# A two-layer hybrid mLSTM / attention kernel: mLSTM scalings moved to ScalarE and joined from PSUM, a front with plain transposes, whole weight quarters and no GpSimd in its norm

## The chip, the cores and the metric

The kernel runs on one core of a Trainium2 chip. Its engines are TensorE (PE in the profile, with its weight loads as PEld), VectorE (DVE), ScalarE (ACT), GpSimd (POOL) and SyncE (SP), which here only issues DMAs. Each engine takes its own instructions in program order and waits on semaphores. The metric is the device time of one execution in microseconds (us); lower is better. Before the change it is 1554.34 us (median of 3 runs, 1553.78 to 1555.73).

## What is computed

Two layers run on 1152 tokens of 1024 features: 1024 latent tokens and 128 context tokens. All arithmetic is float32.

```python
hs = rmsnorm(x, g_pre) * (1 + scale(c)) + shift(c)     # shift, scale, gate = silu(c) @ w_mod + b_mod
# even layer: one projection p = hs @ w_in gives q, k, v, o, gates of 4 mLSTM heads, GQA's q, k, v, and z
h_f = mlstm_scan(q, k, v, ig_f, fg_f)                   # chunks of 128 tokens; h_b the same, reversed
#   in a chunk: P = exp(Dm - m_t) * (q k^T), Dm[l, s] = b_l - b_s + li_s for s <= l, else -inf
#   num = w_inter * (C q) + P v ; den likewise ; h = num / max(|den|, exp(-m_t))
#   C <- a * C + sum_s wk_s v_s k_s^T
ha = rmsnorm(h_f + h_b, g_hn) * sigmoid(o)
y = concat(ha, gqa) * silu(z) ; x = x + gate * rmsnorm(y @ w_out, g_post)
# odd layer: the same frame around neighbourhood attention
```

## The kernel before

**Products.** Projections keep float32 accuracy by splitting each operand into a high and a low part (`hh`, `hl` of the activations; `whi`, `wlo` of the weights) and adding three products in one PSUM bank (lines 371 to 373, 386 to 388, destination `pj`). `split` (line 108) makes the parts: ScalarE casts the high part (line 114), GpSimd or VectorE subtracts it to get the low one (line 115). Tokens lie in three chunks of 384 columns.

**The front** (`run`, from line 1295). The activations come transposed (`xT`, three chunks). For each of 8 feature blocks `mod_first` makes shift and scale: `mod_group` multiplies SiLU(c) by 1 MB of `w_mod` (line 198) and copies the 128x256 result `acc` out of PSUM by `evac`, which takes ScalarE and VectorE in turn (lines 101, 103); two products with a 128x2 selection matrix turn it (line 209); VectorE adds the bias (211, 212). `rms_cols` squares the chunk (290), adds the blocks (297), averages over partitions on TensorE (302), takes the power -1/2 on GpSimd (305) and spreads the row over all partitions by three float32 products with the identity (307). `norm_cols` forms `full` on VectorE (322), `hh` on ScalarE (326) and `hl` on VectorE (327); for the blocks listed in `pool` it takes another way: ScalarE adds the shift (324), ScalarE casts `hh` (114) and GpSimd subtracts (115). While chunk 0 is normalised block by block, the products of the gates (413, 414) and of four weight blocks accumulate in five PSUM banks. The four weight blocks come in quarters of 256 columns: `quarter` issues one DMA for each block (four of 128 KB, line 1332), `cut` splits the four pieces, low parts on GpSimd. SP issues the DMAs in the order of the code: `xT` of chunk 0, `w_mod` of block 0, quarter 0, the gate weights, then `w_mod` of blocks 1 to 7 with a quarter ahead of every second one.

**The mLSTM phase.** A planner of the framework sets the order of each engine's instructions from the code. For each head `mlstm` runs eight state updates: `kw` scales k by a column of `nat`, both directions, on GpSimd (670); TensorE multiplies it with v into the one bank `o` (673); VectorE updates the state `cs` (680). Then come three groups of three chunks. `decays` makes the weights `e` of a group from a broadcast of M: A - M for both directions on GpSimd (653, 128x768), the causal mask on GpSimd (`affine_select`, 656, fill -1e30), exp on ScalarE (658). VectorE multiplies `wb` by q (706) and `e` by the scores (711); TensorE forms the two directions' numerators and denominators in two banks `s` (717, 719); ScalarE takes |den| (725), VectorE floors and inverts it (728, 729), scales both banks into `hs` and `hb` (732, twice 128x384) and adds them (733). ScalarE squares (736), GpSimd takes the root (133, 134) and scales `hs` (739), TensorE transposes it (106), VectorE multiplies by the gate (750). Beside this the projections of the next heads run (`blocks`), and VectorE works off `mods_rest`: 128 reductions of 128x512 (line 252) for the other modulation vectors. The gates of a head: tanh on ScalarE (609), (tanh + 1) * g on GpSimd (610).

**SiLU.** `silu_gate` (390 to 397) makes silu(z) = z * (0.5 * tanh(z/2) + 0.5): tanh on ScalarE (395), the scaling on GpSimd (396), the product on VectorE (397), which frees the PSUM bank `pj` (two of them).

**Softmaxes.** The GQA, neighbourhood and context softmaxes end with a multiplication by 1/sum on GpSimd (924, 1275, 1036).

Of the kernel before, what the change touches and what calls it, by code (L numbers as in the profile page):

```python
# [39 lines left out]
class Kern:  # L40
# [150 lines left out]
    def mod_group(self, ws):  # L191

        nc = self.nc
        pm = self.ps("pj")
        for q, wm in enumerate(ws):
            for kk in range(4):
                b = 32 * kk
                nc.tensor.matmul(pm[b : b + 32, :256], self.cT[:, 4 * q + kk, :], wm[:, kk, :], start=q == 0, stop=q == 1, tile_position=(0, b))
        acc = self.st([P, 256], n="acc")
        self.evac(acc, pm[:, :256])  # L200
        return acc, pm[:, 256:260]

    def mod_first(self, k, ws):

        nc = self.nc
        m = self.mod0[:, k]
        acc, p2 = self.mod_group(ws)
        for j in range(2):
            nc.tensor.matmul(p2[:, 2 * j : 2 * j + 2], acc[:, j * P : (j + 1) * P], self.sel, start=True, stop=True)
# [74 lines left out]
    def rms_cols(self, xt, first=False):  # L284
# [21 lines left out]
        for i in range(3):  # L306
            nc.tensor.matmul(pt[:, i * P : (i + 1) * P], rs[:, i : i + 1].to_broadcast([P, P]), self.ident, start=True, stop=True)
# [4 lines left out]
    def norm_cols(self, h, c, xt, rms, ks, pool=()):

        nc = self.nc
        sh, sc = self.shift[0], self.scale[0]
        for k in ks:
            x, r1 = xt[k // 3][:, k % 3], rms[k > 0 or c > 0]
            f = self.t("full", 4, [P, CW])
            hh, hl = self.act(h, k, c)
            for r, s in ((0, slice(0, CW)),) if c < 2 else ((0, slice(0, 2 * P)), (1, slice(2 * P, CW))):  # L320
                s1, s2 = sc[:, k, r : r + 1], sh[:, k, r : r + 1]
                nc.vector.scalar_tensor_tensor(f[:, s], x[:, s], s1, r1[:, s], ALU.mult, ALU.mult)
                if k in pool:
                    nc.scalar.activation(f[:, s], f[:, s], AF.Identity, bias=s2)
                else:
                    nc.scalar.activation(hh[:, s], f[:, s], AF.Identity, bias=s2)
                    nc.vector.scalar_tensor_tensor(hl[:, s], f[:, s], s2, hh[:, s].bitcast(F32), ALU.add, ALU.subtract)
# [37 lines left out]
    def feat_part(self, ps, h, w, c, ks):  # L365
        nc = self.nc
        whi, wlo = w
        for k in ks:
            hh, hl = self.act(h, k, c)
            a, b = whi[:, k * P : (k + 1) * P], wlo[:, k * P : (k + 1) * P]  # L370
            nc.tensor.matmul(ps[:, :CW], a, hh, start=k == 0, stop=False)  # L371
# [1 line left out]
            nc.tensor.matmul(ps[:, :CW], b, hh, start=False, stop=k == KB - 1)  # L373
# [17 lines left out]
    def silu_gate(self, out, ps):  # L391

        nc = self.nc
        th = self.st([P, CW], n="th")
        nc.scalar.activation(th, ps, AF.Tanh, scale=0.5)
        nc.gpsimd.tensor_scalar(th, th, 0.5, 0.5, ALU.mult, ALU.add)
        nc.vector.tensor_tensor(out, th, ps, ALU.mult)  # L397

# [167 lines left out]
    def mlstm_proj(self, hd):  # L566
# [38 lines left out]
        def oev(c, ps):  # L605
            if c == 0:
                o["g"] = new("gate")
            g = o["g"][:, c * CW : (c + 1) * CW]
# [1 line left out]
            nc.gpsimd.tensor_scalar(g, g, 1.0, self.ghn[:, hd : hd + 1], ALU.add, ALU.mult)  # L610

# [35 lines left out]
    def decays(self, hd, g, t):  # L647

        nc = self.nc
        e, wb = t[:, 0:2], t[:, 2:4]  # L650
# [1 line left out]
        av = self.nat[:, 0, 3 * g : 3 * g + 3, :].rearrange("p c (d h) -> p h d c", d=2)[:, hd]
        nc.gpsimd.tensor_tensor(ev, av[:, :, :, None].to_broadcast([P, 2, 3, P]), ev, ALU.subtract)
        for d in range(2):
            s = 1 if d == 0 else -1
            nc.gpsimd.affine_select(out=ev[:, d], in_=ev[:, d], pattern=[[0, 3], [s, P]], compare_op=ALU.is_ge, fill=NEG, base=0, channel_multiplier=-s)
        ef = e.rearrange("p d l -> p (d l)")
        nc.scalar.activation(ef, ef, AF.Exp)
        return e, wb

    def mlstm(self, hd, cs, order, qT, kT, k, v, gt):
# [4 lines left out]
        def update(chs):  # L666

            kw = self.t("kw", 2, [P, 2, P])
            for d in range(2):
                nc.gpsimd.tensor_tensor(kw[:, d, :], k[:, chs[d], :], nat[:, 1, chs[d], 4 * d + hd : 4 * d + hd + 1].to_broadcast([P, P]), ALU.mult)  # L670
# [32 lines left out]
        for g in range(NC):  # L703
# [25 lines left out]
            nc.vector.reciprocal(den[:, :6], den[:, :6])  # L729
            for d in range(2):  # L730
                pv = po[d][:, : 3 * P1].rearrange("p (c l) -> p c l", l=P1)
                nc.vector.tensor_tensor((hs, hb)[d], pv[:, :, 0:P], den[:, 3 * d : 3 * d + 3, None].to_broadcast([P, 3, P]), ALU.mult)
            nc.vector.tensor_tensor(hs, hs, hb, ALU.add)
# [5 lines left out]
            nc.gpsimd.tensor_tensor(hs, hs, rs[:, :3, None].to_broadcast([P, 3, P]), ALU.mult)
# [282 lines left out]
    def ctx_steps(self, S, V, tmp, po=None, banks=("tr", "s")):  # L1022
# [13 lines left out]
        nc.gpsimd.tensor_tensor(pr, pr, r[:, :2, None].to_broadcast([P, 2, P]), ALU.mult)  # L1036
# [256 lines left out]
    def run(self):  # L1293
# [11 lines left out]
        with self.phase("front"):  # L1305
# [19 lines left out]
            take(0)  # L1325
            raws = [self.raw(), self.raw()] + [self.t(f"raw{b}", 1, [P, D]) for b in range(NB - 2)]
            w = [(self.u([P, D], F32R, "whi"), self.u([P, D], F32R, "wlo")) for _ in range(NB)]

# [25 lines left out]
            for k in range(KB):
# [283 lines left out]
```

## Time and profile before

| | |
|---|---|
| runs | 1554.34 us median, 1553.78 to 1555.73 |
| the profiled execution | 1554.8 us, its span 1553.0 us, mean granted TensorE clock 0.995 |
| busy in the span | PE 1499.3 us, PEld 1380.9, DVE 846.4, ACT 653.0, POOL 609.9 |
| chain that ended last | PE 83% of the span, DVE 6%, DMA 3%, POOL 2%, ACT 2% |
| moved by DMA | 143.80 MB |

Rows of groups read: line, engine, operation, destination<-sources, shapes, count | busy us, mean ns of one | idle time of the engine just before them and what ended most of it. Rows of waits read: engine, destination and line that waited <- engine, destination and line that ended the wait: us in total, times, the longest. Rows of stretches read: from:to in us, length, then for each engine busy us and the number of instructions, the granted clock, the DMA share and GB/s. A busy PE is not PE at its peak, since matmuls are pipelined and their ends are modelled.

### The profile page before, as it was taken

Reading aid. Unit: us, or ns where it says so; the run is one execution under the profiler, and the core shown is the slowest. Engines: PE = TensorE matmul, PEld = TensorE weight load, DVE = VectorE, ACT = ScalarE, POOL = GpSimd, SP = SyncE. Lnnn points to the kernel's source line nnn. Section 1 sums busy time; section 2 is a strip of 40 time slices with the busy share of each in tenths; the row PEclk is TensorE's granted clock in tenths of the full one; section 3 lists DMA queues with packets and bytes.
Section 4 is the critical chain, followed back from the end, with each engine's and each line's share of the span. In section 5 each row is a group of like instructions: output and inputs, shape, how many; then the busy total and the mean of one; then the engine's idle time right before and its main releaser. Section 6 shows DMA issues by size and latency. Waiting matters only on the chain.

```text
span 1553.0 us, 27156 instructions
## 1 busy us (share of the span) xinstructions
PE 1499.3 (97%) x10164; PEld 1380.9 (89%) x10164; DVE 846.4 (55%) x2342; ACT 653.0 (42%) x1573; POOL 609.9 (39%) x830
## 2 busy tenths in 40 slices
PE   7899999999999899999999999999999999999998
PEld 5799998999999888777788989999999999989886
DVE  5732997974547856665465452435243434345532
ACT  4622212112235767778344452445243434345411
POOL 3414645644445835577133332333142314243200
PEclk9999999999999999999999999999999999999999
DMA  9212634431220000021334212131213121225342
GB/s 354 81 42 102 219 124 182 158 113 65 104 93 32 17 23 32 24 72 49 134 108 159 74 52 87 34 105 27 90 44 97 31 84 39 87 76 151 128 130 82
DMA packets 75011, 143.80 MB, mean 93 GB/s; under 512 B 15928, under 2 KB 46848, under 8 KB 74880
## 3 DMA queue, kind: packets, MB, share of 16 engines
q1 hardware_dynamic: 70294, 126.91, 24.7%
q10 hardware_dynamic: 4586, 15.16, 2.6%
q8 instruction: 80, 1.31, 0.3%
q14 instruction: 51, 0.42, 0.1%
HBM read 115.47 MB, written 21.86 MB: 88 GB/s over the span
## 4 chain that ended last, share of the span: by engine, by line
PE 83%; DVE 6%; DMA 3%; POOL 2%; ACT 2%; issue 2%; SPq 0%; DVEq 0%; POOLq 0%; ACTq 0%
PE pj L371 12%; PE pj L373 12%; PE pj L372 12%; PE pj L386 7%; PE pj L387 7%; PE pj L388 7%; PE s L914 4%; PE ptr L106 4%; PE o L954 4%; PE o L1288 4%; PE s L1265 3%; PE tr L106 3%; DVE mj L252 2%; PE pj L106 2%; DMA wm<-in_w_mod_dram 1%
## 5 line engine op out<-in xcount | busy, mean ns | idle before, releaser
L371 PE MATMUL pj<-hh,whi 128*128 128x384 f32 x1168 | 399.9, 342 | 2.9 <-DVE z L397 2.5
L373 PE MATMUL pj<-hh,wlo 128*128 128x384 f32 x1168 | 396.9, 340 | 0.0
L372 PE MATMUL pj<-hl,whi 128*128 128x384 f32 x1168 | 396.0, 339 | 0.0
L371 PEld LDWEIGHTS pj<-hh,whi 128*128 128x128 f32 x1168 | 219.9, 188 | 6.1 <-DVE z L397 2.8
L372 PEld LDWEIGHTS pj<-hl,whi 128*128 128x128 f32 x1168 | 220.0, 188 | 1.3
L373 PEld LDWEIGHTS pj<-hh,wlo 128*128 128x128 f32 x1168 | 219.8, 188 | 1.2 <-issue 0.5
L115 POOL TENSOR_TENSOR wlo<-raw,whi 128x1024 fp32r<-128x1024 f32 (+1 forms) x75 | 156.4, 2096 | 154.6 <-ACT whi L114 105.8
L1275 POOL TENSOR_SCALAR sb<-sb,sm 128x512 f32<-128x512 f32 (+1 forms) x128 | 84.7, 667 | 242.6 <-DVE sm L1274 234.1
L924 POOL TENSOR_SCALAR pr<-pr,smg 128x384 f32<-128x384 f32 x192 | 109.2, 585 | 81.3 <-PE pj L106 41.9
L386 PE MATMUL pj<-whi,hh 128*128 128x256 f32 x432 | 122.5, 284 | 0.3 <-DVE nr L789 0.3
L387 PE MATMUL pj<-wlo,hh 128*128 128x256 f32 x432 | 122.5, 284 | 0.0
L388 PE MATMUL pj<-whi,hl 128*128 128x256 f32 x432 | 122.4, 283 | 0.0
L915 DVE CUSTOM_DVE_ANT_0 pr<-s,zero 128x384 f32<-128x384 f32 x192 | 103.6, 553 | 25.1 <-PE s L914 21.6
L386 PE MATMUL pj<-whi,yh 128*128 128x512 f32 x288 | 114.2, 397 | 2.1 <-DVE o L1083 1.5
L387 PE MATMUL pj<-wlo,yh 128*128 128x512 f32 x288 | 113.8, 395 | 0.0
L388 PE MATMUL pj<-whi,yl 128*128 128x512 f32 x288 | 113.4, 394 | 0.0
L252 DVE CUSTOM_DVE_ANT_0 mj<-wm,cb 128x512 f32<-128x512 f32 x128 | 110.8, 865 | 3.8 <-DMA wm<-in_w_modT_dram 1.8
L1273 ACT ACTIVATE sb<-sb,sm 128x512 f32<-128x512 f32 (+1 forms) x128 | 88.8, 695 | 51.6 <-DVE sm L1271 47.2
L914 PE MATMUL s<-Kst,Q 128*128 128x384 f32 x384 | 107.6, 372 | 0.7 <-DVE smg L915 0.7
L114 ACT CAST whi<-raw 128x1024 fp32r<-128x1024 f32 (+1 forms) x89 | 81.1, 930 | 22.9 <-DMA raw<-in_w_out_dram 6.6
L1271 DVE CUSTOM_DVE_ANT_1 sb<-s,bias 128x512 f32<-128x512 f32 (+1 forms) x112 | 72.9, 664 | 25.0 <-PE ptr L106 14.4
L386 PEld LDWEIGHTS pj<-whi,hh 128*128 128x128 f32 x432 | 81.3, 188 | 1.4 <-issue 0.5
(351 smaller groups left out, 2955.7 us busy)
## 6 DMA issues: line engine op xcount, KB each, us to landing
wm<-in_w_modT_dram SPq DMA_DIRECT2D x32, 512.0 KB, 5.9
raw<-in_w_c_dram SPq DMA_DIRECT2D x25, 512.0 KB, 3.6
raw<-in_w_ab_dram SPq DMA_DIRECT2D x20, 512.0 KB, 3.5
e<-rbd ACTq DMA_DIRECT2D x12, 768.0 KB, 5.5
bias<-in_na_bias_dram SPq DMA_DIRECT2D x16, 576.0 KB, 4.8
wm<-in_w_mod_dram SPq DMA_DIRECT2D x16, 512.0 KB, 7.0
raw<-in_w_out_dram SPq DMA_DIRECT2D x16, 512.0 KB, 3.6
y<-yd SPq DMA_DIRECT2D x18, 448.0 KB, 3.4
```

The source lines that it names most:

```text
L106: self.nc.tensor.transpose(out, in_, self.ident)
L115: (eng_lo or nc.gpsimd).tensor_tensor(lo, src, hi.bitcast(F32), ALU.subtract)
L252: nc.vector.tensor_tensor_reduce(junk, w[:, b, :], cb[:, r, :], 1.0, 0.0, ALU.mult, ALU.add, mp[:, hf, q // 4, 2 * (q % 4) + b, r : r + 1])
L371: nc.tensor.matmul(ps[:, :CW], a, hh, start=k == 0, stop=False)
L372: nc.tensor.matmul(ps[:, :CW], a, hl, start=False, stop=False)
L373: nc.tensor.matmul(ps[:, :CW], b, hh, start=False, stop=k == KB - 1)
L386: nc.tensor.matmul(ps[:, :width], hh, a, start=k == 0, stop=False)
L387: nc.tensor.matmul(ps[:, :width], hh, b, start=False, stop=False)
L388: nc.tensor.matmul(ps[:, :width], hl, a, start=False, stop=k == KB - 1)
L914: nc.tensor.matmul(s[:, :CW], x, y, start=part == 0, stop=part == 1)
L915: nc.vector.tensor_tensor_reduce(pr[:, c, :], s[:, :CW], zero, -1.0, -NEG, ALU.add, ALU.min, m3[:, c : c + 1])
L924: nc.gpsimd.tensor_scalar(pr[:, c, :], pr[:, c, :], r, 1.0, ALU.mult, ALU.mult)
```

## The change

Two sets of edits, in one kernel.

In the mLSTM phase: (1) `decays` gives ScalarE the whole of exp(A - M): six activations of 128x128 with a bias column and scale -1 in place of the one of 128x768, and the mask follows on GpSimd with fill 0. (2) `kw` is made by two ScalarE activations with a scale column. (3) The two directions are joined from PSUM: ScalarE scales the backward one into `hb` (three of 128x128), and VectorE multiplies the forward one and adds `hb` in one operation (three of 128x128). (4) `hs` is scaled by the root on ScalarE (three of 128x128). (5) (tanh + 1) * g becomes one ScalarE activation of 128x384. (6) `silu_gate` leaves out the halving: VectorE multiplies (tanh + 1) by z straight from PSUM, and the factor 0.5 goes into `ghn` (0.25) and into the 1/sum of the three softmaxes; for the context softmax this is one more VectorE operation of 128x2 (`ctx_steps`).

In the front: (7) the products with the selection matrix and with the identity become plain transposes (`flipped`), and the four row groups of the turned `acc` are added by one `tensor_reduce` on VectorE; `acc` is always copied by ScalarE. (8) The four weight blocks are stored in DRAM by quarters (`w_first`), so that one DMA of 512 KB brings a quarter and one cast and one subtraction split it, the subtraction on VectorE. (9) `norm_cols` has no GpSimd way any more.

```diff
 def mod_group(self, ws):
-        self.evac(acc, pm[:, :256])
-        return acc, pm[:, 256:260]
+        nc.scalar.copy(acc, pm[:, :256])
+        return acc, pm[:, 256:]
 def mod_first(self, k, ws):
-            nc.tensor.matmul(p2[:, 2 * j : 2 * j + 2], acc[:, j * P : (j + 1) * P], self.sel, start=True, stop=True)
+            self.flipped(p2[:, j * P : (j + 1) * P], acc[:, j * P : (j + 1) * P])
+        nc.vector.tensor_reduce(m, p2.rearrange("p (j g r) -> p j r g", j=2, r=32)[:, :, 0:2], AX.X, ALU.add)
-        nc.vector.tensor_tensor(m, p2.rearrange("p (b r) -> p b r", r=2), bias, ALU.add)
+        nc.vector.tensor_tensor(m, m, bias, ALU.add)
 def rms_cols(self, xt, first=False):
-            nc.tensor.matmul(pt[:, i * P : (i + 1) * P], rs[:, i : i + 1].to_broadcast([P, P]), self.ident, start=True, stop=True)
+            self.flipped(pt[:, i * P : (i + 1) * P], rs[:, i : i + 1].to_broadcast([P, P]))
 def norm_cols(...):
-                if k in pool:
-                    nc.scalar.activation(f[:, s], f[:, s], AF.Identity, bias=s2)
-                else:
-                    ...
-            if k in pool:
-                self.split(hh, hl, f)
+                nc.scalar.activation(hh[:, s], f[:, s], AF.Identity, bias=s2)
+                nc.vector.scalar_tensor_tensor(hl[:, s], f[:, s], s2, hh[:, s].bitcast(F32), ALU.add, ALU.subtract)
 def silu_gate(self, out, ps):
-        nc.gpsimd.tensor_scalar(th, th, 0.5, 0.5, ALU.mult, ALU.add)
-        nc.vector.tensor_tensor(out, th, ps, ALU.mult)
+        nc.vector.scalar_tensor_tensor(out, th, 1.0, ps, ALU.add, ALU.mult)
 def oev(c, ps):
-            nc.gpsimd.tensor_scalar(g, g, 1.0, self.ghn[:, hd : hd + 1], ALU.add, ALU.mult)
+            nc.scalar.activation(g, g, AF.Identity, scale=self.ghn[:, hd : hd + 1], bias=self.ghn[:, hd : hd + 1])
 def decays(self, hd, g, t):
-        nc.gpsimd.tensor_tensor(ev, av[:, :, :, None].to_broadcast([P, 2, 3, P]), ev, ALU.subtract)
         for d in range(2):
-            nc.gpsimd.affine_select(... fill=NEG ...)
-        nc.scalar.activation(ef, ef, AF.Exp)
+            for i in range(3):
+                nc.scalar.activation(ev[:, d, i], ev[:, d, i], AF.Exp, bias=self.nat[:, 0, 3 * g + i, 4 * d + hd : 4 * d + hd + 1], scale=-1.0)
+            nc.gpsimd.affine_select(... fill=0.0 ...)
 def update(chs):
-                nc.gpsimd.tensor_tensor(kw[:, d, :], k[:, chs[d], :], nat[...].to_broadcast([P, P]), ALU.mult)
+                nc.scalar.activation(kw[:, d, :], k[:, chs[d], :], AF.Identity, scale=nat[...])
 def mlstm(...):
-            for d in range(2):
-                nc.vector.tensor_tensor((hs, hb)[d], pv[:, :, 0:P], den[:, 3 * d : 3 * d + 3, None].to_broadcast([P, 3, P]), ALU.mult)
-            nc.vector.tensor_tensor(hs, hs, hb, ALU.add)
+            for i in range(3):
+                nc.scalar.activation(hb[:, i, :], b, AF.Identity, scale=den[:, 3 + i : 4 + i])
+                nc.vector.scalar_tensor_tensor(hs[:, i, :], f, den[:, i : i + 1], hb[:, i, :], ALU.mult, ALU.add)
...
-            nc.gpsimd.tensor_tensor(hs, hs, rs[:, :3, None].to_broadcast([P, 3, P]), ALU.mult)
+            for i in range(3):
+                nc.scalar.activation(hs[:, i, :], hs[:, i, :], AF.Identity, scale=rs[:, i : i + 1])
 def ctx_steps(...):
+        nc.vector.tensor_scalar(r[:, :2], r[:, :2], 2.0, None, ALU.mult)
 def run(self):
             def quarter(q):
-                for b in range(NB):
-                    nc.sync.dma_start(raws[b][:, o], a["w_ab"][b][:, o])
+                nc.sync.dma_start(raws[q], a["w_first"][q])
             def cut(q):
-                for b in range(NB):
-                    self.split(w[b][0][:, o], w[b][1][:, o], raws[b][:, o])
+                self.split(*w[q], raws[q].rearrange("p (b f) -> p b f", b=NB), eng_lo=nc.vector)
```

The order changes with it. GpSimd's instructions while the first head's output groups are formed (`sm` is the root of the norm, `e` the next head's decays, `wlo` low weights of a projection that runs beside), before:

```order
L656 AFFINE_SELECT e_1557<-e_1557 128x384 x2
L134 TENSOR_TENSOR sm_1553<-sm_1553,mhalf 128x3
L115 TENSOR_TENSOR wlo_1911<-raw_1908,whi_1910 128x1024
L739 TENSOR_TENSOR hs_1540<-hs_1540,sm_1553 128x384
L610 TENSOR_SCALAR gate_1833<-gate_1833,ghn 128x384
L653 TENSOR_TENSOR e_1612<-nat,e_1612 128x768
L133 TENSOR_SCALAR sm_1608<-sm_1604 128x3
```

and after, in the same place (the line numbers are those of the changed file):

```order
L133 TENSOR_SCALAR sm_1522<-sm_1518 128x3
L134 TENSOR_TENSOR sm_1522<-sm_1522,mhalf 128x3
L650 AFFINE_SELECT e_1528<-e_1528 128x384 x2
L115 TENSOR_TENSOR wlo_1892<-raw_1889,whi_1891 128x1024
L650 AFFINE_SELECT e_1588<-e_1588 128x384 x2
L133 TENSOR_SCALAR sm_1582<-sm_1578 128x3
```

GpSimd keeps the root, the mask and the low weights; the scaling of `hs`, the gate and the subtraction of the decays are gone from its queue. ScalarE's instructions in that place, before:

```order
L736 ACTIVATE hb_1541,sm_1549<-hs_1540 128x128 x3
L609 ACTIVATE gate_1833<-pj_1808 128x384
L725 ACTIVATE sm_1594<-s_1580 128x3
L114 CAST whi_1910<-raw_1908 128x1024
L725 ACTIVATE sm_1594<-s_1581 128x3
L644 DMA e_1612<-rbd 128x1536
L658 ACTIVATE e_1557<-e_1557 128x768
L609 ACTIVATE gate_1833<-pj_1842 128x384
```

and after:

```order
L724 ACTIVATE hb_1507<-s_1492,sm_1505 128x128 x3
L687 COPY ct_1473<-tr_1470 128x256
L728 ACTIVATE hb_1507,sm_1518<-hs_1506 128x128
L688 DMA out_dram<-ct_1473 128x2x128
L728 ACTIVATE hb_1507,sm_1518<-hs_1506 128x128 x2
L603 ACTIVATE gate_1814<-pj_1789 128x384
L717 ACTIVATE sm_1565<-s_1551 128x3
L649 ACTIVATE e_1528<-e_1528,nat 128x128 x2
L604 ACTIVATE gate_1814<-gate_1814,ghn 128x384
L649 ACTIVATE e_1528<-e_1528,nat 128x128 x4
L114 CAST whi_1891<-raw_1889 128x1024
L732 ACTIVATE hs_1506<-hs_1506,sm_1522 128x128 x3
```

ScalarE now takes `hb` from PSUM, the exponentials, the gate's scaling and `hs` between the copies (`gate`, `whi`) that it made before. VectorE's instructions in the front, where the first blocks of chunk 0 are normalised, before:

```order
L304 TENSOR_SCALAR sm_267<-ptr_257 128x3
L211 TENSOR_TENSOR mod_109<-pj_232,par 128x4
L212 SCALAR_TENSOR_TENSOR mod_109<-mod_109,par 128x2
L103 COPY acc_292<-pj_283 128x256
L322 SCALAR_TENSOR_TENSOR full_298<-xT_130,mod_109,ptr_257 128x384
L211 TENSOR_TENSOR mod_109<-pj_283,par 128x4
```

and after:

```order
L305 TENSOR_SCALAR sm_256<-ptr_246 128x3
L210 TENSOR_REDUCE mod_109<-pj_220 128x4
L212 TENSOR_TENSOR mod_109<-mod_109,par 128x4
L213 SCALAR_TENSOR_TENSOR mod_109<-mod_109,par 128x2
L115 TENSOR_TENSOR wlo_147<-raw_154,whi_146 128x1024
L323 SCALAR_TENSOR_TENSOR full_282<-xT_130,mod_109,ptr_246 128x384
L210 TENSOR_REDUCE mod_109<-pj_266 128x4
```

VectorE loses the copy of `acc` and gains the reduction and the low part of a whole quarter, ahead of the first `full`.

More of the change, by code (lines that the diff above doesn't have):

```diff
@@ L310, in rms_cols, with norm_cols @@
         return pt[:, :CW], r
-    def norm_cols(self, h, c, xt, rms, ks, pool=()):
+    def norm_cols(self, h, c, xt, rms, ks):
         nc = self.nc
@@ L366, in feat_part @@
         nc = self.nc
-        whi, wlo = w
         for k in ks:
             hh, hl = self.act(h, k, c)
-            a, b = whi[:, k * P : (k + 1) * P], wlo[:, k * P : (k + 1) * P]
+            a, b = (x(k) if callable(x) else x[:, k * P : (k + 1) * P] for x in w)
             nc.tensor.matmul(ps[:, :CW], a, hh, start=k == 0, stop=False)
@@ L651, in decays @@
         ev = e.rearrange("p d (c l) -> p d c l", l=P)
[L652 to L653 removed]
         for d in range(2):
             s = 1 if d == 0 else -1
[L656 to L658 removed]
+            for i in range(3):
+                nc.scalar.activation(ev[:, d, i], ev[:, d, i], AF.Exp, bias=self.nat[:, 0, 3 * g + i, 4 * d + hd : 4 * d + hd + 1], scale=-1.0)
+            nc.gpsimd.affine_select(out=ev[:, d], in_=ev[:, d], pattern=[[0, 3], [s, P]], compare_op=ALU.is_ge, fill=0.0, base=0, channel_multiplier=-s)
         return e, wb
@@ L669, in update @@
             for d in range(2):
-                nc.gpsimd.tensor_tensor(kw[:, d, :], k[:, chs[d], :], nat[:, 1, chs[d], 4 * d + hd : 4 * d + hd + 1].to_broadcast([P, P]), ALU.mult)
+                nc.scalar.activation(kw[:, d, :], k[:, chs[d], :], AF.Identity, scale=nat[:, 1, chs[d], 4 * d + hd : 4 * d + hd + 1])
             pu = self.ps("o")
@@ L729, in mlstm @@
             nc.vector.reciprocal(den[:, :6], den[:, :6])
-            for d in range(2):
-                pv = po[d][:, : 3 * P1].rearrange("p (c l) -> p c l", l=P1)
-                nc.vector.tensor_tensor((hs, hb)[d], pv[:, :, 0:P], den[:, 3 * d : 3 * d + 3, None].to_broadcast([P, 3, P]), ALU.mult)
-            nc.vector.tensor_tensor(hs, hs, hb, ALU.add)
+            for i in range(3):
+                f, b = (po[d][:, i * P1 : i * P1 + P] for d in range(2))
+                nc.scalar.activation(hb[:, i, :], b, AF.Identity, scale=den[:, 3 + i : 4 + i])
+                nc.vector.scalar_tensor_tensor(hs[:, i, :], f, den[:, i : i + 1], hb[:, i, :], ALU.mult, ALU.add)
             ss = self.sm(3)
@@ L1310, in run @@
             self.ghn = self.const([P, 4], "ghn")
-            nc.vector.tensor_scalar(self.ghn, self.par[:, 80:84], 0.5, None, ALU.mult)
+            nc.vector.tensor_scalar(self.ghn, self.par[:, 80:84], 0.25, None, ALU.mult)
             h = [self.chunk("h") for _ in range(NC)]
@@ L1325, in run @@
             take(0)
-            raws = [self.raw(), self.raw()] + [self.t(f"raw{b}", 1, [P, D]) for b in range(NB - 2)]
-            w = [(self.u([P, D], F32R, "whi"), self.u([P, D], F32R, "wlo")) for _ in range(NB)]
+            w = [[self.u([P, NB, 256], F32R, n) for n in ("whi", "wlo")] for _ in range(4)]
+            raws = [self.raw(), self.raw()] + [self.t(f"raw{q}", 1, [P, D]) for q in range(2)]
             def quarter(q):
-                o = slice(256 * q, 256 * q + 256)
-                for b in range(NB):
-                    nc.sync.dma_start(raws[b][:, o], a["w_ab"][b][:, o])
+                nc.sync.dma_start(raws[q], a["w_first"][q])
             def cut(q):
-                o = slice(256 * q, 256 * q + 256)
-                for b in range(NB):
-                    self.split(w[b][0][:, o], w[b][1][:, o], raws[b][:, o])
+                self.split(*w[q], raws[q].rearrange("p (b f) -> p b f", b=NB), eng_lo=nc.vector)
             quarter(0)
@@ L1350, in run @@
             acc = [self.ps("o")] + [self.ps("s") for _ in range(3)] + [self.ps("tr")]
-            part = [gpart] + [lambda ps, c, ks, w=w: self.feat_part(ps, h, w, c, ks) for w in w]
+            block = lambda b: [lambda k, j=j: w[k // 2][j][:, b, k % 2 * P : (k % 2 + 1) * P] for j in range(2)]
+            part = [gpart] + [lambda ps, c, ks, x=block(b): self.feat_part(ps, h, x, c, ks) for b in range(NB)]
             self.mod_first(0, wm[0])
@@ L1365, in run @@
                 if k > 5:
-                    self.norm_cols(h, 1, xt[1], rms[1], range(3 * k - 18, 3 * k - 15), (1, 4))
+                    self.norm_cols(h, 1, xt[1], rms[1], range(3 * k - 18, 3 * k - 15))
             ends = [gend, *evs[:NB]]
@@ L1370, in run @@
             rms.append(self.rms_cols(xt[2]))
-            self.norm_cols(h, 1, xt[1], rms[1], range(6, KB), (6,))
-            self.norm_cols(h, 2, xt[2], rms[2], range(KB), (1, 4, 6))
+            self.norm_cols(h, 1, xt[1], rms[1], range(6, KB))
+            self.norm_cols(h, 2, xt[2], rms[2], range(KB))
             def later(c, bs):
```

7 lines of the change are left out of this document (3 added, 4 removed).

## The prediction

> **What bounds the kernel now.** I read the page's busy line first, then the busy time by stretch of the span, then what TensorE waited for in the stretches that the change touches, then the groups of instructions there. The busy line:
>
> ```profile
> PE 1499.3 (97%) x10164; PEld 1380.9 (89%) x10164; DVE 846.4 (55%) x2342; ACT 653.0 (42%) x1573; POOL 609.9 (39%) x830
> ```
>
> TensorE is the bound: outside its busy time the span of 1553.0 us holds 53.7 us, and no edit shortens its products by much. By stretch (front until the first projection, rest of the front, first projections, mLSTM phase):
>
> ```profile
> 0.00:24.50 24.50, 14.39 (x101) 8.94 (x101) 8.18 (x27) 7.65 (x15) 3.21 (x21) 1.00 0.93 326
> 24.50:80.00 55.50, 50.53 (x342) 42.99 (x339) 44.04 (x90) 32.68 (x69) 26.87 (x26) 1.00 0.44 163
> 80.00:140.00 60.00, 60.00 (x360) 59.18 (x359) 19.75 (x80) 14.16 (x29) 16.23 (x18) 1.00 0.21 74
> 140.00:350.00 210.00, 195.68 (x1232) 190.46 (x1231) 176.12 (x426) 44.45 (x123) 110.80 (x128) 0.99 0.43 152
> ```
>
> The columns behind the length are PE, PEld, DVE, ACT, POOL. TensorE idles 10.1 us in the first stretch (24.50 - 14.39), 5.0 in the second, none in the third and 14.3 in the mLSTM phase. The change acts almost only there, so of the 53.7 us some 29 are all that it can win from waits. What ended most of TensorE's waits in the rest of the front:
>
> ```profile
> PE pj L414 <- POOL hl L115: 3.0, 3, 2.1
> ```
>
> and in the mLSTM phase:
>
> ```profile
> PE pj L371 <- DVE z L397: 2.5, 2, 1.9
> PE o L673 <- POOL kw L670: 2.4, 2, 1.2
> PE tr L106 <- POOL hs L739: 2.1, 2, 1.3
> PE s L717 <- DVE hs L732: 1.7, 1, 1.7
> PE ptr L106 <- ACT k L101: 1.5, 4, 0.6
> PE o L673 <- DVE cs L680: 1.4, 1, 1.4
> ```
>
> Three of these six hang on GpSimd (`z` waits for the halving on line 396): 7.0 us. The others are VectorE's (3.1) and ScalarE's (1.5). VectorE is the second bound here, busy 176 of 210 us; ScalarE has 165 us free.
>
> **The mLSTM phase.** The groups of that stretch:
>
> ```profile
> L252 DVE CUSTOM_DVE_ANT_0 mj<-wm,cb 128x512 f32<-128x512 f32 x128 | 110.8, 865 | 3.8 <-DMA wm<-in_w_modT_dram 1.8
> L670 POOL TENSOR_TENSOR kw<-k,nat 128x128 f32<-128x128 f32 x48 | 24.5, 531 | 62.7 <-PE o L673 62.7
> L653 POOL TENSOR_TENSOR e<-nat,e 128x768 f32<-128x768 f32 x8 | 16.1, 2006 | 8.6 <-DMA e<-rbd 4.8 <-PE pj L373 3.6
> L680 DVE SCALAR_TENSOR_TENSOR cs<-cs,astb,o 128x129 f32<-128x129 f32 x42 | 12.7, 342 | 11.0 <-PE o L673 11.0
> L658 ACT ACTIVATE e<-e 128x768 f32<-128x768 f32 x9 | 7.6, 844 | 29.5 <-POOL e L656 29.5
> L134 POOL TENSOR_TENSOR sm<-sm,mhalf 128x3 f32<-128x3 f32 x7 | 7.6, 1081 | 0.2
> L739 POOL TENSOR_TENSOR hs<-hs,sm 128x384 f32<-128x384 f32 x7 | 6.8, 974 | 0.2
> L736 ACT ACTIVATE hb<-hs 128x128 f32<-128x128 f32 x21 | 6.3, 301 | 16.4 <-DVE hs L733 16.4
> L610 POOL TENSOR_SCALAR gate<-gate,ghn 128x384 f32<-128x384 f32 x6 | 5.9, 978 | 0.2
> L733 DVE TENSOR_TENSOR hs<-hs,hb 128x384 f32<-128x384 f32 x8 | 5.1, 642 | 0.0
> L396 POOL TENSOR_SCALAR th<-th 128x384 f32<-128x384 f32 x6 | 5.0, 842 | 5.7 <-ACT th L395 5.7
> L732 DVE TENSOR_TENSOR hs<-s,sm 128x384 f32<-128x384 f32 x8 | 4.4, 550 | 0.1
> ```
>
> GpSimd loses 24.5 + 16.1 + 6.8 + 5.9 + 5.0 = 58.3 of its 110.8 us. What ScalarE takes instead has no row with a scale column, so I price every 128x128 activation by the nearest, line 736: 0.30 us. That is 48 for `kw` (14.4 us); for eight groups of decays six each, less the one of 0.844 that goes (14.4 - 6.8 = 7.6); three for `hb` and three for `hs` in eight groups (14.4); and six gates of 128x384, which lie between 0.30 and 0.844, taken at 0.5 (3.0). ScalarE rises from 44 to about 84 of 210 us. It isn't full, but its queue is in order, and it also empties the two banks `pj`.
>
> The term by TensorE's waits. `z` (2.5 us) goes whole: tanh and VectorE's product are left. `hs` (2.1): scaling takes 3 x 0.30 in place of 0.97, but GpSimd's root (1.08) stays ahead of it with less in its queue; I take 1.8. `kw` (2.4): 2 x 0.30 in place of 2 x 0.53; half, 1.2. Together 5.5 of 7.0 (bounds 2.5 and 7.0). VectorE's waits (3.1 us) fall as far as VectorE does. The join takes 3 x 0.342 (by line 680, the one row with PSUM, a column and SBUF) in place of 2 x 0.55 + 0.64: 0.7 less, 5.7 us over eight groups. The larger share is what GpSimd does to VectorE's own instructions:
>
> ```profile
> 167.97 2.39 POOL L115 TENSOR_TENSOR wlo<-raw,whi 128x1024 fp32r<-128x1024 f32 x1
> 168.67 2.24 DVE L252 CUSTOM_DVE_ANT_0 mj<-wm,cb 128x512 f32<-128x512 f32 x1
> 172.12 0.69 DVE L252 CUSTOM_DVE_ANT_0 mj<-wm,cb 128x512 f32<-128x512 f32 x1
> ```
>
> The same reduction takes 0.69 us, or 2.24 beside a GpSimd subtraction that ends with it. That subtraction (`wlo`) stays, but with GpSimd's load halved I expect line 252's mean to come down from 865 to about 770 ns (690 at best): 128 x 0.095 = 12 us. VectorE falls from 176 to under 160 us; I take 1.5 of 3.1 (bounds 0 and 3.1). [...]
>
> A wait also costs by the clock. Around the `z` wait:
>
> ```profile
> 200.00:202.00 2.00, 0.10 (x2) 0.01 (x1) 1.47 (x6) 0.00 (x0) 2.00 (x4) 1.00 0.00 0
> 202.00:205.50 3.50, 3.50 (x12) 3.40 (x13) 3.50 (x8) 2.16 (x3) 3.50 (x6) 0.51 0.00 0
> ```
>
> TensorE was idle for 1.9 of 2 us, and then had a granted clock of 0.51 for 3.5 us: 3.5 x 0.49 = 1.7 us of work lost. I book it as won with `z` (else 0; a new wait of this length costs the same). [...]
>
> Against it, waits for ScalarE grow: the row of `k` L101 shows 0.6 us at a time. With twice the load I book 2.0 us more (bounds 0 and 16, first rival). Term: -5.5 - 1.5 - 1.7 + 2.0 = -6.7 us.
>
> **The front.** The rows:
>
> ```profile
> 23.96 0.64 PE L198 MATMUL pj<-wm,cT 128*32 128x256 f32 x8 [0.26 <-DMA wm<-in_w_mod_dram]
> 20.00:40.00 20.00, 19.61 (x153) 15.27 (x153) 14.12 (x25) 12.17 (x27) 11.22 (x14) 1.00 1.03 403
> L115 POOL TENSOR_TENSOR hl<-full,hh 128x384 fp32r<-128x384 f32 x6 | 10.0, 1666 | 20.8 <-ACT hh L114 20.8
> L327 DVE SCALAR_TENSOR_TENSOR hl<-full,mod,hh 128x384 fp32r<-128x384 f32 x13 | 9.9, 770 | 1.7 <-ACT hh L326 1.7
> L103 DVE COPY acc<-pj 128x256 f32<-128x256 f32 x4 | 1.7, 423 | 2.2 <-PE pj L198 2.2
> 16.35 0.16 DVE L304 TENSOR_SCALAR sm<-ptr 128x3 f32<-128x3 f32 x1 [4.96 <-PE ptr L302]
> L115 POOL TENSOR_TENSOR wlo<-raw,whi 128x256 fp32r<-128x256 f32 x16 | 13.2, 863 | 5.9 <-DMA wm<-in_w_mod_dram 5.9
> L307 PE MATMUL ptr<-cc,sm 128*128 128x128 f32 x18 | 3.3, 333 | 0.0
> L209 PE MATMUL pj<-cc,acc 128*128 128x2 f32 x32 | 4.9, 258 | 0.0
> L106 PE MATMUL ptr<-cc,kT 128*128 128x128 f32 x27 | 4.6, 281 | 1.4 <-ACT k L101 0.9 <-DVE k L103 0.4
> ```
>
> The first projection starts at 24.5 us, right behind the product that waits for a `w_mod` DMA. Until then 326 GB/s move, and 403 from 20 to 40 us. Four larger loads in place of sixteen put fewer issues between the `w_mod` loads: nothing at worst, 24.5 x (1 - 326/403) = 4.7 us if the first stretch ran at the later rate; I take 1.5, nearer nothing, since the DMA engines are 93% busy already.
>
> Behind that, the 3.0 us of `hl` waits on GpSimd go, but VectorE gets six `hl` (6 x 0.77 = 4.6 us), four low parts of 1024 columns (bounded by four of line 327's scaled to 1024 columns, 4 x 2.1 = 8.2, and by the 13.2 us that GpSimd took; I take 5, since 0.69 us does for 512 columns above), and eight small reductions (1.3, at the 0.16 us of line 304). It gives up four copies of `acc` (1.7) and the time that GpSimd's 23 us cost it. Its 44.0 of 55.5 us rise to about 50 and leave little slack. I take -2.0 (bounds -5.0, all the idle time of the stretch, and +3.0, VectorE holding TensorE for twice what GpSimd did).
>
> The transposes: L106's 27 records take 4.6 us, 0.17 each. Half of 18 and of 32 records are left: 3.3 - 9 x 0.17 = 1.8 and 4.9 - 16 x 0.17 = 2.2 us saved, a third of it under the DMA wait; I take -1.5 (bounds 0 and -4.0). Front: -1.5 - 2.0 - 1.5 = -5.0.
>
> **The rest.** `silu_gate` outside these stretches ends no wait of TensorE that I book. The doubled sum in `ctx_steps` does lengthen a chain:
>
> ```profile
> PE tr L106 <- POOL pt L1036: 6.1, 4, 2.2
> ```
>
> TensorE waits there four times; one small operation each, 4 x 0.16 = +0.6 (0 to 2, if it shows in all twelve units). The constants 0.5 cost nothing.
>
> **Sum.** -6.7 - 5.0 + 0.6 = -11.1 us. The profiled execution took 1554.8 us (span and 1.8 around it), 0.5 above the median of the runs: 1554.3 - 11.1 = 1543.2, so 1543.
>
> **Rivals.** First, slower: ScalarE's queue becomes the chain. GpSimd stood 62.7 us before `kw` waiting for TensorE to free a buffer (row L670); it could, as little else was queued. Now ScalarE stands there, with the evacuations of `pj` behind it. TensorE has one other bank, a chunk of 24 products at 60.00/360 = 0.17 us (the stretch from 80 us), some 4 us of cover; from a ScalarE wait beyond that TensorE stops. If eight of the 24 update pairs lose 2 us each, +16 in place of +2: 1543 + 14 = 1557. Against it: the placing follows when buffers come free, and ScalarE stood 29.5 us at `e` before without harm. [...] 0.10.
>
> Second: the waits change names only, VectorE being as full behind GpSimd. Then transposes -1.5, clock 0, front -0.5, mLSTM -1.5, `ctx_steps` +0.6: about -3, 1551. For it: VectorE at 176 of 210. 0.15.
>
> Third: VectorE's relief reaches TensorE in full: mLSTM -13 and the clock -1.7, front -9: 1531. For it: 0.69 against 2.24 us. 0.15.
>
> That the change doesn't do what it says I exclude: the listed order shows the instructions gone from GpSimd.
>
> **How the numbers follow.** Forecast 0.60, third rival 0.15, second 0.15, first 0.10. A measurement tells 0.2%, 3.1 us. Faster: 0.60 + 0.15 + half of the second = 0.82; same: the rest of the second and a little of the first, 0.10; slower: 0.08. The range takes in the second rival with the forecast's upper bounds, 1553, and half of the third, 1533.
>
> **What would show it.** Right: no POOL releaser among TensorE's waits from 140 to 350 us, line 252's mean under 800 ns, first projection near 23 us, no half clock near 200 us. Wrong: ScalarE named in new waits of TensorE over 2 us, or `hl` waits on VectorE before 80 us.

## The result, and the profile after

The changed kernel takes 1542.48 us (median of six runs, 1541.04 to 1544.95) against 1555.66 us for the kernel before beside it (six runs, 1553.78 to 1561.55): a ratio of 0.9909, 95% interval 0.9894 to 0.9923, so 13.2 us less. The profiled execution took 1544.44 us, its span 1542.7 us. Ratios here and below are of fast runs alone; one slow execution of `lo_one`, an experiment below, took 2987.3 us and is left out. Line numbers below are those of the changed file unless a row is of another kernel.

The busy line after:

```profile
PE 1497.6 (97%) x10139; PEld 1377.5 (89%) x10139; DVE 828.7 (54%) x2371; ACT 711.1 (46%) x1767; POOL 487.9 (32%) x660
```

GpSimd gave up 122 us and ScalarE took 58; TensorE has the same work in a shorter span. The stretches of the front's rest and of the mLSTM phase after (length, then PE, PEld, DVE, ACT, POOL, granted clock, DMA share, GB/s):

```profile
24.50:80.00 55.50, 50.72 (x323) 42.77 (x316) 43.05 (x103) 29.12 (x55) 4.92 (x3) 0.96 0.40 154
140.00:350.00 210.00, 202.98 (x1295) 197.30 (x1294) 163.76 (x437) 89.15 (x279) 60.75 (x58) 1.00 0.43 156
```

In the mLSTM phase TensorE now idles 7.0 us in place of 14.3. In the front it idles 4.8 in place of 5.0, and its clock there is 0.96. What TensorE waited for after, from 24 to 140 us:

```profile
PE pj L366 <- ACT qT L101: 2.0, 2, 1.6
PE o L407 <- ACT hh L324: 1.5, 1, 1.5
PE pj L408 <- DVE hl L325: 0.8, 1, 0.8
PE o L408 <- DVE hl L325: 0.5, 1, 0.5
```

and in the mLSTM phase:

```profile
PE pj L366 <- DVE z L391: 2.0, 2, 1.4
PE tr L106 <- ACT hs L732: 1.7, 2, 1.0
PE ptr L106 <- ACT k L101: 1.3, 3, 0.6
PE s L711 <- DVE cs L672: 1.1, 1, 1.1
```

No wait names POOL any more and `kw` is gone altogether, but `hs` now waits for ScalarE and `z` is nearly what it was. The groups of the mLSTM phase:

```profile
L253 DVE CUSTOM_DVE_ANT_0 mj<-wm,cb 128x512 f32<-128x512 f32 x128 | 108.8, 850 | 4.1 <-DMA wm<-in_w_modT_dram 2.0
L115 POOL TENSOR_TENSOR wlo<-raw,whi 128x1024 fp32r<-128x1024 f32 x13 | 34.1, 2620 | 112.7 <-ACT whi L114 100.0 <-DVE cf L677 12.7
L662 ACT ACTIVATE kw<-k,nat 128x128 f32<-128x128 f32 x48 | 16.7, 395 | 28.2 <-PE o L665 28.2
L649 ACT ACTIVATE e<-e,nat 128x128 f32<-128x128 f32 x48 | 15.2, 392 | 3.7 <-DMA e<-rbd 3.7
```

A 128x128 activation with a column as scale or bias takes 0.39 us, not 0.30. Line 253 is the disappointment: 850 ns, 15 less than before. For each VectorE instruction between 140 and 350 us I took what it lasted beyond the fastest tenth of its own kind (line, operation and shape; beyond the fastest one where there are under ten), and put the excess down to the GpSimd instruction that overlapped it most. Before, that is 36.0 us, of which 18.6 beside the low parts (`wlo`), 8.5 beside the decays' subtraction and 1.7 beside `kw`. After, it is 24.5, of which 20.2 beside the low parts. On line 253 alone the excess beside them rose from 14.6 to 19.3 us, and that kept its mean high. (The expectations below give smaller sums for this excess, 12.5 of 24.9 us before and 17.9 after; the low parts lead there too.)

One place in the front shows what such a meeting can cost. GpSimd, VectorE and TensorE there:

```profile
71.02 3.21 POOL L115 TENSOR_TENSOR wlo<-raw,whi 128x1024 fp32r<-128x1024 f32 x1 [11.13 <-ACT whi L114]
72.07 2.18 DVE L477 COPY line<-sm 1x4 f32<-1x4 f32 x1
75.00 0.45 PE L366 MATMUL pj<-hh,whi 128*128 128x384 f32 x1 [1.57 <-ACT qT L101]
```

and the clock behind it (the column ahead of the last two):

```profile
76.00:78.00 2.00, 2.00 (x12) 1.96 (x13) 0.00 (x0) 0.00 (x0) 0.00 (x0) 0.52 0.50 203
78.00:80.00 2.00, 2.00 (x8) 1.52 (x7) 0.35 (x2) 0.00 (x0) 0.00 (x0) 0.50 0.00 0
```

A copy of four numbers lasts 2.18 us and ends when GpSimd's subtraction does. Behind it on VectorE stand two thirds of the evacuation of `qT`, for which ScalarE's third waits and which frees a bank `pj`; TensorE stalls 1.57 us, and from 76.1 us runs 6.8 us at half clock. Counting the split products (of which both kernels have 5760), the 161st starts 3.8 us earlier than before, the 201st only 0.1. By the 500th, at 142 us, the lead is 0.4 us; at the 1260th, 10.7.

So my theory for the experiments is that the sum came out by two errors against each other: the front is worth less than 5.0 us and the mLSTM phase more than 6.7, and in both the long subtractions of GpSimd decide. The rivals are the split of the prediction, and ScalarE's or VectorE's queue as the next bound.

### The profile page after: what moved, and what is told of

It reads as the page before. It is cut to its first block, busy times and chain, and to the rows that moved or that the text cites. A ratio compares the mean times of both kernels' runs of the same rounds, so it can differ in the third digit from the quotient of the medians.

```text
span 1542.7 us, 27090 instructions
## 1 busy us (share of the span) xinstructions
PE 1497.6 (97%) x10139; PEld 1377.5 (89%) x10139; DVE 828.7 (54%) x2371; ACT 711.1 (46%) x1767; POOL 487.9 (32%) x660
## 4 chain that ended last, share of the span: by engine, by line
PE 87%; DVE 6%; ACT 2%; issue 2%; DMA 2%; POOL 1%; SPq 0%; DVEq 0%; POOLq 0%; ACTq 0%
PE pj L366 12%; PE pj L367 12%; PE pj L368 12%; PE pj L381 7%; PE pj L382 7%; PE pj L383 7%; PE s L907 4%; PE o L947 4%; PE ptr L106 4%; PE o L1282 4%; PE tr L106 3%; PE s L1259 3%; PE pj L106 2%; DVE mj L253 2%; DMA wm<-in_w_modT_dram 1%
## 5 line engine op out<-in xcount | busy, mean ns | idle before, releaser
L115 POOL TENSOR_TENSOR wlo<-raw,whi 128x1024 fp32r<-128x1024 f32 x59 | 145.2, 2464 | 302.9 <-ACT whi L114 241.8
L114 ACT CAST whi<-raw 128x1024 fp32r<-128x1024 f32 x77 | 79.7, 1045 | 19.5 <-DMA raw<-in_w_v_dram 6.7
```

What stands on the lines that cost most here:

```text
L115: (eng_lo or nc.gpsimd).tensor_tensor(lo, src, hi.bitcast(F32), ALU.subtract)
```

## The experiments

Ratios are to the kernel before on the same chip; 0.001 is 1.56 us. "Idle" is TensorE's idle time from 140 to 350 us, read from that stretch's row as for 7.0 above.

### The two halves alone

Edits 7 to 9 on the kernel before (`front_alone`), and edits 1 to 6 on it (`mlstm_alone`).

> Edits 7 to 9 alone, on the kernel before. By the prediction's terms the front is worth -5.0 us: 1550.7 against 1555.7 (the median of six runs of the kernel before). Theory from the profile after: the front really gains 3.8 us by its 160th product, but in that execution a TensorE stall of 1.7 us at 73 us was followed by 6.8 us of half clock, and 0.1 us was left by 85 us; so 1555 if the half clock comes here too, 1552 if it does not. The granted clock from 76 to 84 us tells which.

> Edits 1 to 6 alone, on the kernel before. By the prediction's terms the mLSTM phase and the context softmax together are worth -6.1 us: 1549.6 against 1555.7. Theory from the profile after: from the 500th product to the 1260th the lag grows from 0.4 to 10.7 us, so these edits bring about -10 us: 1545.6.

The front alone: ratio 0.9984 (0.9971 to 0.9997), -2.5 us. The mLSTM edits alone: 0.9914 (0.9894 to 0.9933), -13.4. The rows of the mLSTM phase, of the front alone:

```profile
76.00:78.00 2.00, 2.00 (x16) 1.73 (x15) 0.00 (x0) 0.00 (x0) 0.00 (x0) 1.00 0.59 229
140.00:350.00 210.00, 191.70 (x1195) 185.56 (x1194) 173.71 (x419) 43.98 (x120) 108.99 (x125) 0.98 0.42 148
```

and of the mLSTM edits alone:

```profile
140.00:350.00 210.00, 203.78 (x1305) 198.95 (x1304) 165.21 (x440) 90.52 (x287) 61.93 (x57) 1.00 0.45 158
```

The same stall of 1.57 us stands at 74 us in the front alone, without a half clock behind it, and its lead of 2.7 us lasts to the 500th product. Its mLSTM phase then idles 18.3 us, 4.0 more than before, and runs 6.8 us at half clock from 147 us, where the kernel before has 3.4 at 202 us. TensorE's instructions come in the same order there as before; why the earlier arrival meets longer waits is not shown. (Its profiled execution, 1558.75 us, lies above the median of its twelve runs, 1556.54.) The interval of the front alone, -4.5 to -0.5 us, takes in both values that I expected, -3.7 without the half clock and -0.7 with it. The mLSTM edits gained more than the 10 us expected, and their profiled span is 12.0 us shorter than before's. The split of the prediction falls: half of the front's term, twice the mLSTM's.

### The low parts off GpSimd

```diff
 def blocks(hd, evs, bs, new=None):
-                w = self.weights(a["w_ab"][5 * hd + b], new=new)
+                w = self.weights(a["w_ab"][5 * hd + b], new=new, vec="lo")
```

`lo_all` has this on the kernel after; `lo_one` only for the one weight block of the first head, prepared at 71 us; `lo_before` has it on the kernel before, without the change.

> The kernel after, with one low part (128x1024, the weight block prepared at 71 us) subtracted on VectorE in place of GpSimd. Theory: GpSimd's subtraction from 71.02 to 74.23 us held VectorE's 1x4 copy for 2.18 us, by that the copies of qT and gT behind it, by that TensorE for 1.6 us, and that stall brought the half clock of 76 to 83 us (3.4 us of work). With it gone the stall is under 1 us and the clock stays full: 1542.5 - 4 = 1538.5. Rival: VectorE's own 1.2 us stands ahead of the same copies and the stall and the half clock stay: 1542.5.

> The kernel after, with all low parts of the head projections' weights (128x1024, 13 of them between 140 and 350 us) on VectorE in place of GpSimd. Theory: beside these subtractions VectorE's instructions lost 17.9 us of that stretch (line 253 17.1); VectorE takes 13 x 1.22 = 16 us instead, so that its busy time stays near 164 us, line 253's mean falls from 850 to about 700 ns, no VectorE instruction is held for over 1 us, and TensorE's waits for z and cs get shorter: 1536 to 1539. Rival: the low parts stand ahead of chain work in VectorE's queue and TensorE waits longer for z and the weights: 1545.

> The kernel before with one edit: the low parts of the head projections' weights on VectorE in place of GpSimd, nothing else of the change. Theory (what holds TensorE in the mLSTM phase is VectorE held by GpSimd's long subtractions): 12.5 of the 24.9 us that VectorE's instructions lost beside GpSimd go, VectorE takes 12 x 1.22 = 15 us, TensorE's 14.3 idle us from 140 to 350 us fall to about 9: ratio 0.997 to the kernel before. Rival (VectorE's queue is the bound, busy 176 of 210 us): it rises to 178 or more and the time stays or grows, ratio 1.000 to 1.003.

`lo_one`: ratio 0.9895 (0.9874 to 0.9916), not told apart from the kernel after by the runs, but its trace shows the hold. TensorE's wait for `qT`, and the clock:

```profile
PE pj L366 <- ACT qT L101: 1.2, 2, 0.8
```

```profile
76.00:78.00 2.00, 2.00 (x14) 1.70 (x14) 0.06 (x1) 0.00 (x0) 0.00 (x0) 1.00 0.47 190
```

The copies of four numbers take 0.15 us each, the stall is 0.8 us, and no half clock follows. So the hold of VectorE made half of the stall. That it brought the half clock is not shown, since four runs with the whole stall of 1.57 us have none there either. `lo_all`: 0.9856 (0.9836 to 0.9875), 1536.46 us, below the interval of the kernel after. Its reductions and low parts, and its stretch:

```profile
L253 DVE CUSTOM_DVE_ANT_0 mj<-wm,cb 128x512 f32<-128x512 f32 x128 | 89.1, 696 | 5.3 <-DMA wm<-in_w_modT_dram 3.0
L115 DVE TENSOR_TENSOR wlo<-raw,whi 128x1024 fp32r<-128x1024 f32 x13 | 16.2, 1244 | 2.8 <-ACT whi L114 2.8
```

```profile
140.00:350.00 210.00, 207.19 (x1326) 204.27 (x1327) 162.50 (x459) 95.14 (x296) 31.82 (x47) 0.99 0.45 160
```

VectorE took over 16.2 us of work and is busy 162.5 us against 163.8: the subtraction costs it less than standing beside it did. Idle falls to 2.8 us. `lo_before`: 0.9983 (0.9967 to 0.9998), idle 9.6 us with two half-clock windows, at 148 and 288 us: right in direction, but the low parts alone are worth little as long as the decays, `kw` and the other scalings stay on GpSimd.

### One edit put back

The kernel after, with one edit undone: `kw` (edit 2), the halving (6), the decays (1). `lo_z_back` undoes the halving in `lo_all`.

> The kernel after with kw scaled on GpSimd again, as before. By the prediction's term (half of 2.4 us) +1.2. Theory: GpSimd gets 24.5 us back, both waits for kw (2.4 us) return and the roots wait behind it: TensorE's idle time from 140 to 350 us rises from 7.0 to 10 or more, +3. Rival (ScalarE's queue matters): ScalarE loses 16.7 us, the waits for hs and k on ScalarE (3.0 us) get shorter, and the time falls by 1.

> The kernel after with the halving of silu_gate on GpSimd again (and the three softmaxes and the gate's constant as before). By the prediction's terms +2.5 for z, and +1.7 if a half clock follows: +2.5 to +4.2. Theory from the profile after, where the z waits are still 2.0 us, on VectorE held by GpSimd's low parts: the GpSimd step adds its own 0.8 us to two waits, +1 to +1.5.

> The kernel after with the decays as before: GpSimd's subtraction of 128x768 (2 us, one per group) and the mask ahead of one exp on ScalarE. The prediction had no wait of TensorE on it, only a share of VectorE's relief: +0.5. Theory: GpSimd gets 16 us back, of which VectorE's instructions lose about 5, the roots wait behind it, and a wait for e or hs grows: +2 to +4, ratio 0.993. Rival (ScalarE's queue matters): six short activations less per group outweigh it: 0 to -2.

> As lo_all (low parts of the head projections on VectorE), with silu_gate's halving on GpSimd again. In the kernel after, putting that halving back cost 0.5% (0.9959 against 0.9909), twice the prediction's 2.5 to 4.2 us. Theory (the halving is dear because it waits in GpSimd's queue behind low parts of 2.6 us and VectorE is held by them): with these off GpSimd it costs under 3 us against lo_all: ratio 0.986 to 0.988. Rival (the halving is dear by itself, as one more step in the chain that frees a PSUM bank): again 8 us, ratio 0.991.

| | ratio (95%) | idle us | half-clock windows, 140 to 350 us | against 0.9908 |
|---|---|---|---|---|
| after again | 0.9908 (0.9887 to 0.9929) | 7.2 | 0 | |
| `kw` back | 0.9933 (0.9916 to 0.9950) | 11.4 | 0 | +3.9 us |
| halving back | 0.9959 (0.9944 to 0.9975) | 12.2 | 2 | +7.9 |
| decays back | 0.9986 (0.9970 to 1.0003) | 16.2 | 3 | +12.1 |
| `lo_all`, halving back | 0.9855 (0.9832 to 0.9879) | 2.7 | 0 | -8.3 |

`kw` went as the theory had it, though its interval overlaps that of the changed kernel, so its 3.9 us is less sure than the rest. The other two cost far more than it said: 7.9 us for 1 to 1.5, and 12.1 for 2 to 4. Part of that is the clock, which the theory left out: a half-clock window of 3.4 us costs 1.7 us of work (clock 0.51 for 3.5 us at 202 us in the kernel before), so 3.4 of the 7.9 and 5.1 of the 12.1. TensorE's waits with the decays back:

```profile
PE tr L106 <- ACT hs L734: 3.2, 3, 1.6
PE pj L368 <- POOL wlo L115: 2.9, 1, 2.9
PE o L667 <- DVE cs L674: 2.6, 3, 1.2
PE pj L366 <- DVE z L391: 2.5, 3, 1.4
PE ptr L106 <- ACT kT L584: 1.9, 1, 1.9
```

None names the decays, but GpSimd's queue shows them ahead of the low part for which TensorE waits 2.9 us:

```profile
278.40 2.17 POOL L647 TENSOR_TENSOR e<-nat,e 128x768 f32<-128x768 f32 x1 [6.38 <-DMA e<-rbd]
280.53 2.78 POOL L115 TENSOR_TENSOR wlo<-raw,whi 128x1024 fp32r<-128x1024 f32 x1
```

The high part of that weight was ready at 276.1 us. GpSimd stood idle for the decays' DMA until 278.4, then subtracted for 2.17 us, and only then came the low part. `cs` and `z` on VectorE, `hs` and `kT` on ScalarE have longer waits too. The three costs add up to 23.9 us, more than the whole change is worth: they are not terms of a sum, since each fills the same queue. The last row shows the same from the other side: with the low parts off GpSimd the halving costs nothing that the runs can tell (0.9856 and 0.9855).

One rival stays untested. The planner gives most of these kernels another order of instructions: TensorE's departs from that of the changed kernel at 81 us in `lo_all`, at 110 with the halving back, at 132 with `kw` back or done twice, and at 181 with the decays back. No run changes an edit and keeps the order, so a part of each cost, and of the gain of `lo_all`, may be the order's.

### ScalarE loaded twice

```diff
 def update(chs):
             for d in range(2):
                 nc.scalar.activation(kw[:, d, :], k[:, chs[d], :], AF.Identity, scale=...)
+                nc.scalar.activation(kw[:, d, :], k[:, chs[d], :], AF.Identity, scale=...)
```

> The kernel after with every scaling of kw on ScalarE done twice, one after the other (same output): 48 more activations of 0.395 us, 19 us more in the mLSTM phase, ScalarE 89 to 108 of 210 us. It doubles the load on which the first rival rests. First rival (ScalarE's queue is near to being the chain): each of 28 updates comes 0.8 us later and TensorE's waits for kw, k and hs grow to over 10 us: +8 or more. Theory (ScalarE has slack, it stood 28 us ahead of kw waiting for TensorE): waits grow by under 3 us, +1 to +3.

Ratio 0.9949 (0.9933 to 0.9966), +6.4 us against 0.9908: nearer the rival's 8 than my 1 to 3. TensorE's longest wait there:

```profile
PE s L710 <- ACT hb L725: 3.3, 1, 3.3
```

Idle is 11.7 us, with half clock at 147 and 267 us, which takes 3.4 us. The waits that name ScalarE add up to 5.0 us against 3.0 in the kernel after, not to over 10, and none is for `kw`; the others name VectorE. So ScalarE's 121 idle us were no measure of its slack, as the first rival had it, but the waits that the rival named grew little, and the way to the 6.4 us is shown in part only.

### The changed kernel again, and a faster one

`lo_ctx` is `lo_all` with one more edit, in `ctx_steps`:

```diff
-        nc.vector.tensor_scalar(r[:, :2], r[:, :2], 2.0, None, ALU.mult)
         nc.vector.reciprocal(r[:, :2], r[:, :2])
-        nc.gpsimd.tensor_tensor(pr, pr, r[:, :2, None].to_broadcast([P, 2, P]), ALU.mult)
+        for hh in range(2):
+            nc.vector.tensor_scalar(pr[:, hh, :], pr[:, hh, :], r[:, hh : hh + 1], 0.5, ALU.mult, ALU.mult)
```

> The kernel after, unchanged. Its execution of the result had 6.8 us of half clock at 76 us; four later kernels with the same front and the same stall of 1.57 us at 73 us had none. Theory (a stall of 1.4 to 1.9 us is followed by half clock or not, by how it falls on a grid of 3.41 us): ratio near 0.991 again, with or without the half clock at 76 us; if without, its span is about 3 us below 1542.7. Rival (this program always has it): half clock at 76 us again.

> As lo_all, with the context softmax's scaling on VectorE (two of 128x128, the factor 0.5 in the same operation) in place of a doubling on VectorE and a multiplication on GpSimd (0.61 us). TensorE waits 4 times, 6.2 us in all, for that GpSimd step in lo_all. Theory: about 0.5 us less at each of the 4 waits, so -2 us against lo_all, ratio 0.984, and no POOL among these waits. Rival: VectorE is held there by the row maxima, the waits change their name only: ratio 0.9856 as lo_all.

The changed kernel again: 1544.5 us, ratio 0.9908, and its half clock at 76 us is there again, for 6.8 us. That goes with my rival for this run; with the decays back it came too, for 3.4 us, and in four others with the same stall it did not. `lo_ctx`: 1530.14 us (1528.77 to 1532.65), ratio 0.9819 (0.9795 to 0.9842), the fastest kernel here, 14 us below the kernel after on the same chip. The wait on which it acts, in `lo_all`:

```profile
PE tr L106 <- POOL pt L1030: 6.2, 4, 2.2
```

and in `lo_ctx`:

```profile
PE tr L106 <- DVE pt L1030: 1.8, 1, 1.8
```

I expected 2 us and it was 5.8 (0.9856 - 0.9819): three of the four waits are gone whole, not just the 0.61 us of the operation, and the half clock at 890 us is not in its trace. The two intervals touch (0.9836 and 0.9842), so how much of the 5.8 is this edit's is less sure than its sign.

## Why the prediction was right, point by point

The time, 1543 against 1542.5, and the sum, -11.1 against -13.2, were right; the terms were not, so the closeness is luck. The front was booked too high, the mLSTM phase too low, and the kernel before, at 1555.66 us beside the changed one, was 1.3 us slower than the runs I started from. Of the signs of being right three came (no wait that names POOL from 140 to 350 us, the first projection at 23.1 us, no half clock near 200 us), and the fourth, line 252 under 800 ns, did not.

- **DMA start, -1.5:** right. The first projection comes at 23.1 us, 1.4 earlier.
- **Waits for `hl`, -2.0:** the step that failed in the front. The 3.0 us on GpSimd went, but 2.8 us at ScalarE's `hh` and VectorE's `hl` took their place, and 2.0 at `qT`; idle time moved from 5.0 to 4.8 us. The sign named as wrong, `hl` waits on VectorE before 80 us, did appear, and the 2.0 us at `qT` stand at the edge of the other one.
- **Transposes, -1.5:** by the 161st product the lead is 3.8 us; without the start 2.4 are left for transposes and waits together, where 3.5 were booked. No run parts the two.
- **A new wait of that length costs the clock:** written for the gap of 1.9 us at 200 us, it came at 76 behind a stall of 1.57 us, where it took 3.4 us back; of seven runs with that stall, three had it.
- **GpSimd's waits in the mLSTM phase, -5.5:** the sum of 7.0 fell to 3.7 (`z` 2.0 and `hs` 1.7), so -3.3. Whole for `kw` (2.4, I took half), little for `z` (0.5, I took all), 0.4 for `hs` (I took 1.8).
- **VectorE's waits, -1.5:** 1.3 us for `cs` are left of 3.1, so -1.8. But the step behind it failed: line 252 was to fall to 770 ns and fell to 850, since the low parts, which stayed on GpSimd, and not the 58 us taken off it, hold it (19.3 us of excess). The 12 us that VectorE gained came from the join (13.9 to 8.3 us) and from shorter other operations (line 706, now 698, from 1537 to 954 ns).
- **Half clock at 200 us, -1.7:** right for the kernel after, which has none from 140 to 350 us.
- **New waits for ScalarE, +2.0:** the 1.7 us at `hs` are those of the 3.7 above, and `k` has slightly less, so nothing came on top: booked too high at this load. `kw_twice` shows how close the bound is (+6.4 us against the kernel after).
- **The mLSTM term, -6.7:** mis-sized, and the largest error. The trace after has 7.3 us less idle time in the stretch and no half clock (1.7), which makes 9.0. Alone these edits measure -13.4 with the context softmax in them. I priced each edit by the waits that one trace names. The decays, which no wait named, are worth most when put back. In the trace of the mLSTM edits alone, 8.1 us less idle time and the half clock at 202 us (1.7) make 9.8 of the 10.9 us by which that kernel gets faster from the 500th split product to the last numerator (279.7 to 268.8 us).
- **`ctx_steps`, +0.6:** TensorE's wait for GpSimd there went from 6.1 to 4.8 us and one of 1.7 for ScalarE came; from the mLSTM's last numerator to the end both executions take 1131 us. Nothing, as near as can be told.
- **The rivals:** the second (names change only) describes the front; the third's -13 for the mLSTM phase is what was measured, though not through line 252. Its full relief of VectorE came with `lo_all`.

What VectorE lost beside GpSimd differs by the instruction: in the kernel after 20.2 us beside the 34.1 of the long subtractions, where a copy of four numbers took 2.18 us in place of 0.15; in the kernel before 1.7 us beside the 24.5 of `kw`, so little of `kw`'s time could come back there.

## What to carry to other kernels

When an edit takes work off an engine's queue, price the queue and not the waits that name the edit: find the longest instructions in it, and see what they hold up on the other engines. Then test by moving the long ones, which here was worth some 8 us (0.9908 to 0.9856), the planner's new order included. A sum that comes out does not show that its terms do; two runs of the halves do.

## What the runs showed of the hardware

**The half clock kept a grid in these traces.** In 14 executions the stretches of half clock (granted clock 0.50) ahead of the kernel's end last 3.41 or 6.83 us, and the full ones ahead of them whole multiples of 3.41 (54.6, 447.1 and 191.2 us in the kernel after, 180.9, 334.5 and 361.8 in the one before). I divided each execution into windows of that grid and added up TensorE's idle time in each that ran at full clock, after the first 20 us. All 27 windows with 1.88 us or more of it were followed by half clock; of 55 between 1.42 and 1.88 us, 15; none of 32 between 1.30 and 1.42. So one and the same stall of 1.57 us was charged 1.7 us or 3.4 or nothing. What decides between 1.42 and 1.88 us stays open; of the seven stalls of 1.57 us at 73 us, the three that were followed began 0.3 to 0.8 us into their window, the four others 1.3 to 2.0.

**VectorE held by GpSimd for a few numbers.** A copy of 1x4 took 2.18 us beside a subtraction of 128x1024 on GpSimd, and 0.15 us with that on VectorE. The subtraction itself takes 2.6 us on GpSimd and 1.24 on VectorE.
